# Bias rows stored from ScalarE's queue, with new priorities of a planned order, in a transformer block on one core

## The chip, the cores and the metric

The kernel runs on one core of a Trainium2 chip. The metric is the device time of one execution in microseconds. A core has TensorE (PE, matmuls and transposes), VectorE (DVE), ScalarE (ACT), GpSimd (POOL) and SyncE (SP); SP does nothing here but issue DMA transfers. ACT and POOL can issue transfers too.

## The reference

One layer on a sequence of 512 tokens with 1024 features, in float32. A first product with `w_in` gives the inputs of two attentions: MLA with low-rank latents, and NSA with compressed, selected and sliding branches. Then follow the output product, a gated FFN and a last norm.

```python
u = rmsnorm(h, norm_mix_g[l]) @ w_in[l]
c_q, c_kv, k_rope, q_nsa, kv_cmp, kv_slc, kv_win, gate_logits = jnp.split(u, cuts, axis=-1)
o_mla = mla_mixer(c_q, c_kv, k_rope, ...)
o_nsa = nsa_mixer(q_nsa, kv_cmp, kv_slc, kv_win, gate_logits, ..., t5_table)
mixed = jnp.concatenate([rmsnorm(o_mla, ...), rmsnorm(o_nsa, ...)], axis=-1)
h = h + mixed @ w_out[l]
f = rmsnorm(h, norm_ffn_g[l])
h = h + (jax.nn.silu(f @ w_gate[l]) * (f @ w_up[l])) @ w_down[l]
```

In NSA each head adds a bias to its scores that depends on the distance of query and key alone; it is looked up in `t5_table`, 32 buckets by 8 heads. The bias rows of this document are that lookup. The compressed branch makes 31 keys and values per group by a small network, `gelu(blk @ w1) @ w2`, over windows of 32 tokens.

## The kernel before, in words

**Arithmetic.** Each float32 operand is split into a high and a low part (`split`, `split_pieces`), and a product is three matmuls (`mm3`, L167 to L170): high by high, low by high, high by low. A weight tile is therefore loaded (`w_raw`), cast to its high part (`w_hi`, L391) and subtracted to its low part (`w_lo`, L393 on DVE or L394 on POOL) before PE can use it. `weight` (L396) does this: there are two buffers for `w_raw` and three for the parts, so a load waits until the tile two before it is split.

**Stages.** x and the weights of the latents come first; x is normed and transposed in four blocks of 128 tokens (`xTh`, `xTl`), and each block gives its latents (`latent`, L461), the matmuls of 440 columns. Then come the projections from x with 512 columns: keys (two, k0 and k1), queries (four, q0 to q3), the raw inputs of the compressed keys and values, and the values. For the compressed keys and values, pieces of the projection go to `rr`, the hidden layer is a product with two tiles of `w1` (L715, L717), its sum passes through `hs` and `z` (L728 to L748) to `hth` and `htl` (L391, L393), and these meet `w2h`. The softmax of the heads follows, then MLA, the output product and the FFN.

**The bias rows.** `bias_rows` (L529) multiplies `choice`, a one-hot table of buckets, with the split `t5_table` (`tx`, split into `txp`), negates the result into `brow` (L539) and stores it in DRAM. Two stores of 8 x 32 x 320 values, the row of each head written 32 times, make `ldr` (L543, 320 KB each); two small ones make `gdr` (L545). From there the rows are loaded again, skewed: `bn` for each pair of heads in four loads (L595), and `ga` for the compressed branch in eight (L603). All these go through SP's queue.

**The order.** Nothing is left to a scheduler at run time: `Plan` (L74) is given jobs with an engine, an estimated time, the jobs that they follow, a priority, and the buffers that they take and free. `run` places each job on its engine in its own model of time, the lower priority number first among those that could start at once, and emits the instructions in that order. The numbers in `PRI` (L123) shift the priorities of whole groups. So a small change of a number moves instructions on several engines. `sum_weights` (L1344) adds tiles of `w_down` for the FFN beside all this: ACT issues a copy into T (L1356), POOL an accumulating transfer onto it (L1357).

The queries' results (`qs`) leave their PSUM bank by ACT (high part) and DVE (low part, L370); there are two such banks, named mm.

Of the kernel before, what the change touches and what calls it, by code (L numbers as in the profile page):

```python
# [13 lines left out]
OP = mybir.AluOpType  # L14
# [9 lines left out]
H = 8  # L24
# [30 lines left out]
class Plan:  # L55
# [11 lines left out]
    def add(self, ways, fn=None, after=(), pri=0.0, takes=(), frees=(), lag=None):  # L67

        if fn is not None:
            ways = [(ways[0], ways[1], fn)]  # L70
        j = Job(ways, [a for a in after if a is not None], pri, takes, frees, lag)
        self.jobs.append(j)
        return j
# [13 lines left out]
    def run(self):  # L87
        busy = {}
        clock, ready, waiting = {"dma": 3500.0, "dma2": 3000.0}, [], list(self.jobs)
        while waiting or ready:  # L90
# [29 lines left out]

PRI = dict(k0=-28.1, q0=-12.1, v=-4.9, ck=-13.0, k1=8.9, cv=-9.5, q1=-9.4, q2=57.6, q3=12.2, mla=56.1, out=231.6, slack=0, pdve=18.6, ppool=86.3,  # L123
           pact=287.7, wload=-5.7, wsplit=39.6, mkeys=-41.5, lat=-40.5, cmp=-18.2, cuse=34.2, use=6.8, sout=44.8, seven=181.5, xoff=-24.0,
           xstep=-81.5, loff=-30.6, woff=-18.0, wstep=8.6)


@with_exitstack
def block_kernel(ctx: ExitStack, tc: tile.TileContext, I, out):
    nc = tc.nc  # L130
    ve, se, pe, gp, sy = nc.vector, nc.scalar, nc.tensor, nc.gpsimd, nc.sync
# [103 lines left out]
    ldr = dram.tile([H, 32, 640], F32, name="ldr")  # L235
    gdr = dram.tile([H, 1008], F32, name="gdr")
# [21 lines left out]
    tx = p0.tile([33, H], F32, name="tx")  # L258
    choice = kqv.tile([33, 1648], F32R, name="choice", tag="kl")
    txp = p0.tile([33, 2, H], F32R, name="txp")  # L260
# [2 lines left out]
        q.dma_start(xt[0][:, 512 * e:512 * e + 512], xv[:, 0, 512 * e:512 * e + 512])  # L263
    se.dma_start(grow, I["norm_mix_g"].unsqueeze(0))
    ve.memset(tx, -BIG)


    order = tc.manual_schedule(engines={e.engine for e in (ve, se, pe, gp)})
# [2 lines left out]
    add = plan.add  # L271
# [117 lines left out]
    def split_pieces(h, l, raw, n, after, pri, takes=(), frees=()):  # L389

        j = add([("act", t_act(n, True), lambda: se.copy(h(), raw())), ("dve", t_copy(n), lambda: ve.tensor_copy(h(), raw()))],  # L391
                None, after, pri, takes=takes)
        return add([("dve", t_dve(n), lambda: ve.tensor_tensor(l(), raw(), f(h()), op=OP.subtract)),  # L393
                    ("pool", t_pool(n), lambda: gp.tensor_tensor(l(), raw(), f(h()), op=OP.subtract))], None, [j], pri, frees=frees)  # L394
# [32 lines left out]
    g_row = add(("dma2", 20), lambda: None, pri=-99, lag=600)  # L427
# [6 lines left out]
    wl_ready = []  # L434
    for u in range(4):
        j = add(("dma", 1300), lambda u=u: load_wl(u), pri=-97 + (u if u < 3 else 4), lag=950)
# [6 lines left out]
    def load_small():  # L443
        sy.dma_start(rc, I["rope_c"].rearrange("(t p) d -> p t d", p=P))
        sy.dma_start(rs, I["rope_s"].rearrange("(t p) d -> p t d", p=P))
        sy.dma_start(rowv, I["row_valid"])
        sy.dma_start(tx[0:32, :], I["t5_table"])
        sy.dma_start(og[:, 0:4], I["out_norm_mla_g"].rearrange("(k p) -> p k", p=P))
        sy.dma_start(og[:, 4:8], I["out_norm_nsa_g"].rearrange("(k p) -> p k", p=P))

    small = add(("dma", 2100), load_small, pri=-89.5, lag=950)
    choice_in = add(("pool", 1010), lambda: gp.dma_start(choice, I["bias_choice"]), pri=-89.5, lag=3400)
# [76 lines left out]
    def bias_rows(c0, c1):  # L529
        d = {}  # L530

        def product():
            d["o"] = bank("tp")
            for e in range(2):
                pe.matmul(d["o"][0:H, 0:c1 - c0], txp[:, e], choice[:, c0:c1], start=e == 0, stop=e == 1)

        def negated():
            d["row"] = pa.tile([H, S], F32, name="brow", tag="s", bufs=4)[:, 0:c1 - c0]
            se.mul(d["row"], d["o"][0:H, 0:c1 - c0], -1.0)  # L539

        def out():
            if c1 <= 640:
                sy.dma_start(ldr[:, :, c0:c1], d["row"].unsqueeze(1).to_broadcast([H, 32, 320]))  # L543
            else:
                sy.dma_start(gdr[:, c0 - 640:c1 - 640], d["row"])  # L545

        j = add(("pe", (c1 - c0) * 0.834), product, [table, choice_in], -60, takes=["tp"])
        choice_used.append(j)
        j = add(("act", t_act(c1 - c0)), negated, [j], -60, takes=["s"], frees=["tp"])
        return add(("dma", 950 if c1 <= 640 else 100), out, [j], -60, frees=["s"], lag=4300)  # L550

    table = split_pieces(lambda: txp[:, 0], lambda: txp[:, 1], lambda: tx, H, [small], -60)
    choice_used = []
    bias0 = [bias_rows(0, 320), bias_rows(320, 640)]
    bias1 = [bias_rows(640, 1144), bias_rows(1144, 1648)]
# [526 lines left out]
    for t in range(NT):  # L1082
        d = {}
# [6 lines left out]
        j = add(("pe", 640), go, uv_ready + lat_done, mpri + t, takes=["mm"])  # L1090
        vm_ready += split_values(lambda t=t: late["vm"][:, t], lambda d=d: d["o"].rearrange("p (h d) -> p h d", h=H), S, [j], mpri + t)
    for q in range(2):
        qc = slice(384 * q, 384 * q + 384)
        for t in range(NT):
            pri = mpri + 4 + 4 * q + t
            d = {}
# [15 lines left out]
            j = add(("pe", 480), lambda go=go: go(0), [uq_ready[q][0]] + lat_done, pri, takes=["mm"])  # L1112
            j = add(("pe", 480), lambda go=go: go(1), [j, uq_ready[q][1]], pri)
            j = add(("act", t_act(256)), lambda qd=qd, ov=ov: se.copy(qd()[:, :, 0:64], ov()[:, :, 0:64]), [j], pri)
            j = add(("dve", 480), rope, [j], pri, frees=["mm"])
# [192 lines left out]
    for nh in range(2):  # L1308
        for t in range(NT):
            d = {}  # L1310
# [14 lines left out]
    for nh in range(2):  # L1325
        for t in range(NT):
            d = {}
# [6 lines left out]
            j = None  # L1334
            for k in range(4):
                j = add(("pe", 640), lambda k=k, go=go: go(k), [j, wo[4 + 2 * nh + k // 2][1][k % 2]] + latent_jobs, 300 + 4 * nh + t,
                        takes=["mm"] if k == 0 else (), frees=["part2"] if t == NT - 1 and k % 2 else ())
# [6 lines left out]
    def sum_weights():  # L1344
        wd = I["w_down"].rearrange("(q j p) (n c) -> p q j n c", j=2, p=P, n=2)
        last = [ga_loaded]
        for u in range(6):
            qs = slice(2 * u, min(2 * u + 2, 11))
            n = qs.stop - qs.start
            for name in ("T1", "T3", "T2", "T4"):  # L1350
                wsum[name, u] = dram.tile([P * n, 512], F32, name=f"{name}_{u}")
            b = lambda jj, nn, qs=qs: wd[:, qs, jj, nn, :]
            o = lambda name, u=u: wsum[name, u].rearrange("(q p) c -> p q c", p=P)
            for name, first, second in (("T1", lambda b=b: b(0, 0), lambda b=b: b(0, 1)), ("T3", lambda b=b: b(1, 1), lambda b=b: b(0, 1)),
                                        ("T2", lambda b=b: b(0, 0), lambda o=o: o("T3")), ("T4", lambda b=b: b(1, 0), lambda o=o: o("T2"))):
                j = add(("act", 80), lambda o=o, name=name, first=first: se.dma_start(o(name), first()), last, 900, lag=8000)  # L1356
                j = wsum_done[name, u] = add(("pool", 1000), lambda o=o, name=name, second=second: gp.dma_start(o(name), second(), accum_op=OP.add, max_dma_last_dim=2048), [j], 900, lag=8500)  # L1357
                last = [j]

    sum_weights()  # L1360
# [580 lines left out]
```

## Time and profile before

| | before |
|---|---|
| time, median of 3 runs | 654.06 us (652.67 to 654.91) |
| the profiled execution | 651.38 us, span 649.6 us |
| mean granted TensorE clock | 0.983 of full |
| PE busy | 611.7 us, 94% of the span |
| DVE busy | 524.7 us, 81% |
| ACT busy | 370.0 us, 57% |
| POOL busy | 175.9 us, 27% |
| chain that ended last | PE 76%, DVE 14% |

The span runs from the first to the last instruction; the execution is some 1.8 us longer. Busy time is time in instructions of the engine itself; issues of transfers are rows of the engine's queue (SPq, ACTq). Overlapping matmuls are drawn with their modelled ends, so a row's length is more than the distance to the next one. In a timeline, the bracket at the end of a row gives the idle time ahead of it and what ended it.

### The profile page before, as it was taken

What the parts mean: (1) busy time and instruction counts of PE and PEld (TensorE: products, weight loads), DVE (VectorE), ACT (ScalarE), POOL (GpSimd) and SP (SyncE); (2) the same over time, 40 slices, a digit from 0 to 9 for tenths busy, and PEclk for the clock granted to TensorE, in tenths of its full rate; (3) what the DMA queues carried; (4) which work ended last, traced back from release to release, by engine and by line L of the source; (5) the groups of instructions that cost most, each with busy time, mean ns of one, the idle gap of its engine ahead of it and who ended that gap; (6) DMA issues with size and microseconds to landing.
All of it is one profiled execution on the core that took longest, in us unless ns stands there. A gap on an engine that the chain in (4) does not pass through costs nothing.

```text
span 649.6 us, 11224 instructions
## 1 busy us (share of the span) xinstructions
PE 611.7 (94%) x3973; PEld 543.9 (84%) x3973; DVE 524.7 (81%) x1078; ACT 370.0 (57%) x766; POOL 175.9 (27%) x253
## 2 busy tenths in 40 slices
PE   5998599998998999999999999999999999999994
PEld 3877488887897777787999999999999998888883
DVE  5947377799999888858987778977778899978846
ACT  4532134798898877526644554455455576558434
POOL 5622236356975475434100000000000000000003
PEclk9999789999999989999999999999999999999998
DMA  8526564327323555456775775557553466455503
GB/s 277 133 52 136 144 153 93 63 68 179 65 35 70 185 173 123 101 154 197 170 201 160 195 190 135 138 156 195 163 149 108 112 212 199 146 174 191 186 1 130
DMA packets 76297, 92.75 MB, mean 143 GB/s; under 512 B 10240, under 2 KB 49584, under 8 KB 76242
## 3 DMA queue, kind: packets, MB, share of 16 engines
q1 hardware_dynamic: 63856, 68.22, 34.7%
q0 software_dynamic: 6080, 11.75, 11.6%
q10 hardware_dynamic: 6306, 12.06, 5.8%
q8 instruction: 31, 0.51, 0.3%
q14 instruction: 24, 0.20, 0.1%
HBM read 89.24 MB, written 25.85 MB: 177 GB/s over the span
## 4 chain that ended last, share of the span: by engine, by line
PE 76%; DVE 14%; issue 3%; ACT 3%; DMA 1%; POOL 1%; SPq 1%; POOLq 0%; ACTq 0%; DVEq 0%
PE mm L168 10%; PE mm L169 10%; PE mm L170 10%; PE sc L170 7%; PE sc L169 7%; PE sc L168 7%; PE pv L879 3%; PE pv L170 3%; PE pv L169 3%; PE pv L168 3%; PE tp L845 3%; PE sc L1185 2%; PE tp L169 2%; PE tp L170 2%; PE tp L168 2%
## 5 line engine op out<-in xcount | busy, mean ns | idle before, releaser
L170 PE MATMUL sc<-fh,w_unit 128*128 128x256 f32 x352 | 98.5, 280 | 0.0
L168 PE MATMUL sc<-fh,w_unit 128*128 128x256 f32 x352 | 98.5, 280 | 0.0
L169 PE MATMUL sc<-fl,w_unit 128*128 128x256 f32 x352 | 98.2, 279 | 0.0
L1396 DVE TENSOR_TENSOR w_unit<-b_raw,w_unit 128x1024 fp32r<-128x1024 f32 (+1 forms) x54 | 63.8, 1182 | 25.5 <-ACT w_unit L1580 15.2
L169 PEld LDWEIGHTS sc<-fl,w_unit 128*128 128x128 f32 x352 | 66.2, 188 | 0.0
L170 PEld LDWEIGHTS sc<-fh,w_unit 128*128 128x128 f32 x352 | 66.1, 188 | 0.0
L168 PEld LDWEIGHTS sc<-fh,w_unit 128*128 128x128 f32 x352 | 65.8, 187 | 0.0
L834 ACT ACTIVATE s<-s,m 128x128 f32<-128x128 f32 (+3 forms) x96 | 53.5, 558 | 11.3 <-DVE m L829 10.5
L1396 DVE TENSOR_TENSOR w_unit<-b_first,w_unit 128x1024 fp32r<-128x1024 f32 (+1 forms) x34 | 40.0, 1176 | 24.6 <-ACT w_unit L1580 18.2
L840 POOL TENSOR_SCALAR s<-s,l,gates 128x128 f32<-128x128 f32 (+3 forms) x64 | 41.4, 658 | 32.2 <-DVE l L837 24.8
L170 PE MATMUL mm<-fh,w_unit 128*128 128x256 f32 x176 | 49.3, 280 | 0.0
L168 PE MATMUL mm<-fh,w_unit 128*128 128x256 f32 x176 | 49.1, 279 | 0.0
L169 PE MATMUL mm<-fl,w_unit 128*128 128x256 f32 x176 | 49.1, 279 | 0.0
L853 DVE TENSOR_TENSOR ptl<-tp,pth 128x128 fp32r<-128x128 f32 (+3 forms) x96 | 45.2, 484 | 3.9 <-ACT pth L850 3.2
L394 POOL TENSOR_TENSOR w_lo<-w_raw,w_hi 128x512 fp32r<-128x512 f32 x25 | 35.0, 1413 | 39.7 <-DVE w_hi L391 29.9
L850 ACT ACTIVATE pth<-tp 128x128 fp32r<-128x128 f32 (+3 forms) x96 | 40.4, 432 | 7.1 <-PE tp L845 6.0
L845 PE MATMUL tp<-ident,s 128*128 128x128 f32 x240 | 41.9, 280 | 2.3 <-DVE ptl L853 1.1
L1580 ACT CAST w_unit<-b_raw 128x1024 fp32r<-128x1024 f32 x32 | 33.6, 1051 | 11.8 <-issue 4.8
L1357 POOL DMA_DIRECT2D T<-T x12 | 13.2, 1100 | 100.0 <-DMA T<-in_w_down_dram 99.7
L1357 POOL DMA_DIRECT2D T<-in_w_down_dram x12 | 13.5, 1121 | 93.9 <-DMA T<-in_w_down_dram 93.9
L845 PEld LDWEIGHTS tp<-ident,s 128*128 128x128 f32 x240 | 29.0, 142 | 9.9 <-POOL s L840 4.2
L1856 POOL TENSOR_SCALAR ss<-ss 128x1 f32<-128x1 f32 x9 | 3.4, 376 | 123.3 <-ACT xo L1853 123.0
(365 smaller groups left out, 1986.1 us busy)
## 6 DMA issues: line engine op xcount, KB each, us to landing
T<-in_w_down_dram ACTq DMA_DIRECT2D x20, 512.0 KB, 5.1
b_first<-in_w_gate_dram SPq DMA_DIRECT2D x12, 512.0 KB, 4.7
b_raw<-in_w_up_dram SPq DMA_DIRECT2D x12, 512.0 KB, 6.6
T<-in_w_down_dram POOLq DMA_DIRECT2D x10, 512.0 KB, 6.4
T<-T POOLq DMA_DIRECT2D x10, 512.0 KB, 5.9
b_raw<-in_w_gate_dram SPq DMA_DIRECT2D x10, 512.0 KB, 3.9
b_late<-in_w_up_dram SPq DMA_DIRECT2D x10, 512.0 KB, 5.2
b_raw<-in_w_down_dram SPq DMA_DIRECT2D x10, 512.0 KB, 3.9
```

The lines of the kernel that those rows point to most:

```text
L168: pe.matmul(o, lh, rh, start=start, stop=False, **kw)
L169: pe.matmul(o, lh, rl, start=False, stop=False, **kw)
L170: pe.matmul(o, ll, rh, start=False, stop=stop, **kw)
L394: ("pool", t_pool(n), lambda: gp.tensor_tensor(l(), raw(), f(h()), op=OP.subtract))], None, [j], pri, frees=frees)
L834: se.activation(c["s"][:, 0:n], c["s"][:, 0:n], AF.Exp, bias=c["m"], scale=-1.0, accum_out=c["l"])
L840: eng.tensor_scalar(c["s"][:, 0:n], c["s"][:, 0:n], c["l"], gate(), op0=OP.mult, op1=OP.mult)
L845: pe.transpose(c["tp"][:, j * P:(j + 1) * P], c["s"][:, j * P:(j + 1) * P], ident)
L850: se.activation(c["dh"], c["src"], AF.Copy)
L853: ve.tensor_tensor(c["dl"], c["src"], f(c["dh"]), op=OP.subtract)
L1357: j = wsum_done[name, u] = add(("pool", 1000), lambda o=o, name=name, second=second: gp.dma_start(o(name), second(), accum_op=OP.add, max_ ...
L1396: return add(("dve", t_dve(n)), lambda: ve.tensor_tensor(dst(), a(), b(), op=op), after, pri, **kw)
L1580: j = add(("act", t_act(n, True)), lambda: se.copy(w["p"][0], b()), [rw] + need, pri + 5)
```

## The change

- `t5_table` is loaded by ACT at the start instead of by SP among the small loads, and its split no longer waits for those loads.
- The four stores of bias rows are issued by ACT (`se`) instead of SP (`sy`). In the plan each is a job of ACT, which also follows the split of the latents' weights.
- The priorities in `PRI` are replaced; those of the bias rows and of `sum_weights` become entries of it.
- The plan reckons PE's jobs below 1374 ns as 7% longer.

```diff
@@ -67,7 +67,7 @@ def add(self, ways, fn=None, after=(), pri=0.0, takes=(), frees=(), lag=None):
-            ways = [(ways[0], ways[1], fn)]
+            ways = [(ways[0], ways[1] * (1.07 if ways[0] == "pe" and ways[1] < 1374 else 1.0), fn)]
@@ -120,9 +120,9 @@
-PRI = dict(k0=-28.1, q0=-12.1, v=-4.9, ck=-13.0, k1=8.9, cv=-9.5, q1=-9.4, q2=57.6, q3=12.2, mla=56.1, out=231.6, slack=0, pdve=18.6, ppool=86.3,
...
+PRI = dict(k0=-5.4, q0=-12.1, v=51.3, ck=-13.0, k1=8.0, cv=-9.5, q1=-9.4, q2=-38.5, q3=12.6, mla=38.1, out=180.9, slack=0, pdve=20.1,
...
+           xoff=-26.6, xstep=-35.5, bias=-61.8, sums=912.1, bout=-82.5, loff=-25.8, woff=-217.5, wstep=301.5)
@@ -263,6 +263,7 @@
     ve.memset(tx, -BIG)
+    se.dma_start(tx[0:32, :], I["t5_table"])
@@ -444,7 +445,6 @@
-        sy.dma_start(tx[0:32, :], I["t5_table"])
@@ -540,16 +540,16 @@
         def out():
             if c1 <= 640:
-                sy.dma_start(ldr[:, :, c0:c1], d["row"].unsqueeze(1).to_broadcast([H, 32, 320]))
+                se.dma_start(ldr[:, :, c0:c1], d["row"].unsqueeze(1).to_broadcast([H, 32, 320]))
             else:
-                sy.dma_start(gdr[:, c0 - 640:c1 - 640], d["row"])
+                se.dma_start(gdr[:, c0 - 640:c1 - 640], d["row"])
 
-        j = add(("pe", (c1 - c0) * 0.834), product, [table, choice_in], -60, takes=["tp"])
+        j = add(("pe", (c1 - c0) * 0.834), product, [table, choice_in], PRI["bias"], takes=["tp"])
         choice_used.append(j)
         j = add(("act", t_act(c1 - c0)), negated, [j], -60, takes=["s"], frees=["tp"])
-        return add(("dma", 950 if c1 <= 640 else 100), out, [j], -60, frees=["s"], lag=4300)
+        return add(("act", 80), out, [j] + wl_ready, PRI["bout"], frees=["s"], lag=6000)
 
-    table = split_pieces(lambda: txp[:, 0], lambda: txp[:, 1], lambda: tx, H, [small], -60)
+    table = split_pieces(lambda: txp[:, 0], lambda: txp[:, 1], lambda: tx, H, [g_row], PRI["bias"])
@@ -1353,8 +1353,8 @@
-                j = add(("act", 80), lambda o=o, name=name, first=first: se.dma_start(o(name), first()), last, 900, lag=8000)
...
+                j = add(("act", 80), lambda o=o, name=name, first=first: se.dma_start(o(name), first()), last, PRI["sums"], lag=8000)
...
```

Lines 266 to 447 of the file before are one higher after the change; the rest keeps its number. No matmul is added or left out. From the mask and `w_out` on SP's order is that of before, and from the FFN's first transposes on PE's is.

On SP, between the hidden weights of the compressed keys and those of the values. Before (`w_raw<-in_w_in` is a tile of the projections):

```order
L404 DMA w_raw<-in_nsa_cmp_w_k_dram 128x8x128 x2
L543 DMA ldr<-brow 256x1x320 x2
L545 DMA gdr<-brow 8x504 x2
L404 DMA w_raw<-in_w_in_dram 128x8x128
L595 DMA bn<-ldr 32x2x512 x8
L603 DMA ga<-gdr 16x8x56 x8
L404 DMA w_raw<-in_w_in_dram 128x8x128
L404 DMA w_raw<-in_nsa_cmp_w_v_dram 128x8x128 x2
```

After the change:

```order
L405 DMA w_raw<-in_nsa_cmp_w_k_dram 128x8x128 x2
L595 DMA bn<-ldr 32x2x512 x8
L405 DMA w_raw<-in_w_in_dram 128x8x128
L603 DMA ga<-gdr 16x8x56 x8
L405 DMA w_raw<-in_w_in_dram 128x8x128
L405 DMA w_raw<-in_nsa_cmp_w_v_dram 128x8x128 x2
```

The four stores are gone from here, and the `bn` loads stand ahead of the tile of the compressed values. The tile behind the `ga` loads is that of q1 in both.

On ACT, among the norms of x (`x_109`) and the first latents. Before:

```order
L321 ACTIVATE xTh,ss<-x_109 128x4x128 x2
L362 ACTIVATE xTh<-tp 128x4x128
L321 ACTIVATE xTh,ss<-x_109 128x4x128
L362 ACTIVATE xTh<-tp 128x4x128 x2
L475 ACTIVATE cn,css<-mm 128x256
L476 ACTIVATE cn,css<-mm 128x128
L478 ACTIVATE ge<-mm 128x24
```

After the change:

```order
L322 ACTIVATE xTh,ss<-x_109 128x4x128
L543 DMA ldr<-brow 256x1x320
L322 ACTIVATE xTh,ss<-x_109 128x4x128
L363 ACTIVATE xTh<-tp 128x4x128 x2
L475 ACTIVATE cn,css<-mm 128x256
L476 ACTIVATE cn,css<-mm 128x128
L478 ACTIVATE ge<-mm 128x24
L539 ACTIVATE brow<-tp 8x320
L543 DMA ldr<-brow 256x1x320
L363 ACTIVATE xTh<-tp 128x4x128
L392 CAST w_hi<-w_raw 128x512 x2
```

Both `ldr` stores now lie here, the second ahead of a piece of x and of the first casts of projection tiles; the two `gdr` stores follow behind the last latents.

On DVE, around the hidden layer of the compressed keys. Before:

```order
L393 TENSOR_TENSOR w_lo<-w_raw,w_hi 128x512
L370 SCALAR_TENSOR_TENSOR qs<-mm,qs 64x512 x2
L689 TENSOR_SCALAR rr<-ident 128x8x2x4 x2
L391 CAST w_hi<-w_raw 128x512
L732 TENSOR_TENSOR hs<-mm,hs 128x68
L734 TENSOR_SCALAR z<-hs 128x64
L737 TENSOR_TENSOR hs<-z 128x2x32
```

After the change:

```order
L394 TENSOR_TENSOR w_lo<-w_raw,w_hi 128x512
L371 SCALAR_TENSOR_TENSOR qs<-mm,qs 64x512
L392 CAST w_hi<-w_raw 128x512
L371 SCALAR_TENSOR_TENSOR qs<-mm,qs 64x512
L394 TENSOR_TENSOR w_lo<-w_raw,w_hi 128x512
L689 TENSOR_SCALAR rr<-ident 128x8x2x4 x2
L732 TENSOR_TENSOR hs<-mm,hs 128x68
L734 TENSOR_SCALAR z<-hs 128x64
```

Of the low part's two halves of q0 (`qs`), the second now stands behind the cast of a tile, q1's. On PE the projections come in the order q2, compressed keys, q0, compressed values, q1, k0, k1, q3, values; before it was k0, compressed keys, q0, compressed values, q1, values, k1, q2, q3, with the softmax mixed in from the values on. The two small bias products stand before the transposes of x and in the first latents, where they stood behind the last latents.

## Rows read from the trace of the kernel before

**Rows 1.** The page, part 1: busy us, share of the span, instructions.

```profile
PE 611.7 (94%) x3973; PEld 543.9 (84%) x3973; DVE 524.7 (81%) x1078; ACT 370.0 (57%) x766; POOL 175.9 (27%) x253
```

**Rows 2.** Windows by stage: length; busy PE, PEld, DVE, ACT, POOL; PEclk; DMA share, GB/s.

```profile
16.00:39.00 23.00, 21.41 (x122) 19.27 (x122) 19.74 (x52) 11.08 (x35) 11.28 (x15) 1.00 0.46 117
...
62.00:92.00 30.00, 20.93 (x94) 17.11 (x94) 15.80 (x37) 5.92 (x17) 9.05 (x8) 0.77 0.56 137
92.00:312.00 220.00, 209.60 (x1297) 178.16 (x1297) 189.40 (x590) 154.26 (x427) 123.02 (x185) 0.99 0.47 121
312.00:630.00 318.00, 317.25 (x2286) 298.10 (x2285) 263.27 (x321) 173.21 (x225) 12.45 (x12) 1.00 0.56 159
```

**Rows 3.** Timeline of PE: start, length, line, operation, [idle before <- releaser].

```profile
64.22 0.76 PE L168 MATMUL mm<-xTh,w_hi 128*128 128x512 f32 x1 [1.86 <-DVE qs L370]
...
67.34 0.44 PE L169 MATMUL mm<-xTl,w_hi 128*128 128x512 f32 x1
...
78.01 0.39 PE L168 MATMUL mm<-hth,w2h 128*128 128x64 f32 x1 [6.88 <-DVE hth L391]
...
79.19 0.77 PE L168 MATMUL mm<-xTh,w_hi 128*128 128x512 f32 x1
...
84.45 0.42 PE L170 MATMUL mm<-xTh,w_lo 128*128 128x512 f32 x1
```

**Rows 4.** Timeline of SP: start and total time of the DMA issues.

```profile
40.85 1.62 SPq L543 DMA_DIRECT2D ldr<-brow  x2
43.39 8.07 SPq L545 DMA_DIRECT2D gdr<-brow  x2
51.57 3.70 SPq L404 DMA_DIRECT2D w_raw<-in_w_in_dram  x1
56.67 8.09 SPq L595 DMA_DIRECT2D bn<-ldr  x8
64.80 3.74 SPq L603 DMA_DIRECT2D ga<-gdr  x8
68.66 0.39 SPq L404 DMA_DIRECT2D w_raw<-in_w_in_dram  x1
```

**Rows 5.** Waits of SP's queue, 14 to 80 us: total, times, longest.

```profile
SPq L595 <- DMA T<-in_w_down_dram: 4.6, 1, 4.6
```

**Rows 6.** DMA from 38 to 60 us: rate in 0.55 us slices; issues, KB each, landing.

```profile
GB/s 0 0 0 0 0 0 0 14 54 44 49 54 42 54 42 51 47 49 51 42 54 44 49 47 49 51 72 54 44 49 49 47 62 145 323 342 356 177 209 216
...
w_raw<-in_w_in_dram SPq DMA_DIRECT2D x1, 512.0 KB, 8.5
...
T<-in_w_down_dram ACTq DMA_DIRECT2D x1, 512.0 KB, 4.0
```

**Rows 7.** Timeline of ACT: two stretches of it.

```profile
24.11 0.61 ACT L391 CAST w_hi<-w_raw 128x512 fp32r<-128x512 f32 x1
...
53.46 1.55 ACT L362 ACTIVATE rr<-mm 64x256 fp32r<-64x256 f32 x4 [1.23 <-PE mm L170]
...
59.01 0.69 ACTq L1356 DMA_DIRECT2D T<-in_w_down_dram  x1
```

**Rows 8.** The chain that ended last, pieces in order of time: start, length, what.

```profile
44.10 0.33 PE tp L504 x3
...
46.39 0.23 PE mm L170
...
68.66 4.02 DMA w_raw<-in_w_in_dram
...
83.37 0.43 PE mm L170
```

**Rows 9.** DMA from 14 to 36 us: rate in forty slices of 0.55 us.

```profile
GB/s 308 177 28 1 16 75 275 343 338 304 290 279 63 0 0 0 0 0 0 0 0 0 30 0 0 106 243 344 325 246 287 266 77 23 19 0 2 141 209 340
```

**Rows 10.** DMA from 60 to 82 us: issues, KB each, median landing.

```profile
T<-in_w_down_dram POOLq DMA_DIRECT2D x1, 512.0 KB, 7.0
w_raw<-in_w_in_dram SPq DMA_DIRECT2D x2, 256.0 KB, 6.5
```

More of the change, by code (lines that the diff above doesn't have):

```diff
@@ L119, in run @@
         self.jobs = []
-PRI = dict(k0=-28.1, q0=-12.1, v=-4.9, ck=-13.0, k1=8.9, cv=-9.5, q1=-9.4, q2=57.6, q3=12.2, mla=56.1, out=231.6, slack=0, pdve=18.6, ppool=86.3,
-           pact=287.7, wload=-5.7, wsplit=39.6, mkeys=-41.5, lat=-40.5, cmp=-18.2, cuse=34.2, use=6.8, sout=44.8, seven=181.5, xoff=-24.0,
-           xstep=-81.5, loff=-30.6, woff=-18.0, wstep=8.6)
+PRI = dict(k0=-5.4, q0=-12.1, v=51.3, ck=-13.0, k1=8.0, cv=-9.5, q1=-9.4, q2=-38.5, q3=12.6, mla=38.1, out=180.9, slack=0, pdve=20.1,
+           ppool=72.3, pact=310.9, wload=-10.3, wsplit=-28.4, mkeys=-2.4, lat=-20.5, cmp=-18.4, cuse=94.3, use=17.0, sout=77.2, seven=183.9,
+           xoff=-26.6, xstep=-35.5, bias=-61.8, sums=912.1, bout=-82.5, loff=-25.8, woff=-217.5, wstep=301.5)
 @with_exitstack
@@ L1355, in sum_weights @@
                                         ("T2", lambda b=b: b(0, 0), lambda o=o: o("T3")), ("T4", lambda b=b: b(1, 0), lambda o=o: o("T2"))):
-                j = add(("act", 80), lambda o=o, name=name, first=first: se.dma_start(o(name), first()), last, 900, lag=8000)
-                j = wsum_done[name, u] = add(("pool", 1000), lambda o=o, name=name, second=second: gp.dma_start(o(name), second(), accum_op=OP.add, max_dma_last_dim=2048), [j], 900, lag=8500)
+                j = add(("act", 80), lambda o=o, name=name, first=first: se.dma_start(o(name), first()), last, PRI["sums"], lag=8000)
+                j = wsum_done[name, u] = add(("pool", 1000), lambda o=o, name=name, second=second: gp.dma_start(o(name), second(), accum_op=OP.add, max_dma_last_dim=2048), [j], PRI["sums"], lag=8500)
                 last = [j]
```

## The prediction

> **What bounds the kernel now.** I read the page's engine totals first. PE is busy 611.7 us of a span of 649.6 [rows 1], so the question is where the other 38 us lie and which of them this change can reach. The windows by stage answer it [rows 2]. From 312 to 630 us PE works 317.25 of 318 us at the full clock; nothing can be won there unless matmuls go away, and none does. From 92 to 312 us, where the softmax stands, PE idles 220 - 209.60 = 10.4 us while DVE is busy 189.40. The stretch from 62 to 92 us is the bad one: PE works 20.93 of 30 us, and at a mean granted clock of 0.77.
>
> PE's timeline says what happens in that stretch [rows 3]. PE waits 1.86 us for a bank that DVE has to empty (`qs`), and after the projection of the compressed values it waits 6.88 us for `hth`, the hidden layer of the compressed keys. With a short third wait of 0.33 us these are the stretch's 30 - 20.93 = 9.07 us. After either wait the matmuls run at the lower level of the clock, 1.2 GHz. The chain shows 0.43 us for a matmul of 512 columns there and 0.23 us at 2.4 GHz [rows 8]. The first slow spell lasts from 64.22 to 67.34 us, 3.12 / 0.43 = 7 matmuls, which lose 0.20 us each: 1.45 us. The second, from 79.19 to 84.45 us, loses 5.26 / 0.43 x 0.20 = 2.45 us. **The stretch loses 9.07 + 1.45 + 2.45 = 13.0 us.**
>
> Why is `hth` late? Not for its own work. On DVE the cast of the next weight tile, that of q1, stands ahead of the steps that make `hth`, and the tile came late. The chain runs through its transfer: issued at 68.66 us, 4.02 us long [rows 8], landed at 72.7 us, and `hth` reaches PE at 78.01 us [rows 3], 5.3 us behind it. SP's timeline tells why it was issued so late [rows 4]. Two `ldr` stores go out at 40.85 us; the two `gdr` stores behind them hold SP for 8.07 us although they are small; the tile after them holds it 3.70 us, where a free issue takes 0.39 us. Then eight `bn` loads hold it 8.09 us, in which the fifth waits 4.6 us for a transfer T that it does not read [rows 5]: transfers share a set of completion counters in turn, and the issue waits until the counter's last user has landed. Eight `ga` loads take 3.74 us, 0.47 us each. While the stores drain, from 42 to 55 us, the DMA engines move some 42 to 54 GB/s, and the tile issued at 51.57 us lands only after 8.5 us [rows 6].
>
> **The change, part by part.**
>
> *Stores off SP's queue.* SP loses four issues, and with them the holds behind them. In the new order the `bn` loads follow the two halves of the compressed keys' hidden weights. They can go once the last latent block is through, at 44.10 + 0.33 = 44.4 us [rows 8]. An issue takes (8.09 - 4.6) / 8 = 0.44 us [rows 4, 5], so all eight are out by 47.9 us if the stores have landed by then. The next tile, the compressed values', goes between 47.9 and 51.6 us, since its buffer comes free as before. Four `ga` loads follow. The fifth `ga` load now waits for the first T, which is the wait to watch. T stands on ACT behind the four `rr` pieces, which end at 53.46 + 1.55 = 55.0 us, and lands 4.0 us later [rows 6, 7]: 59.0 us. Four more issues of 0.47 us give 60.9 us for the tile of q1, against 68.66 us. With the same 4.02 us it lands at 64.9 us, **7.8 us earlier**.
>
> *What is late next.* DVE's new order puts the second low half of `qs` behind the cast of that tile; before, it stood ahead of it. This half empties the bank that the compressed values' projection takes. So this wait grows: tile 64.9 us, plus about 0.43 us for the cast and 0.6 us for `qs` (an estimate from ACT's 0.61 us for a piece of that size [rows 7]), gives 66.0 us, and PE has been out of work since 64.22 - 1.86 = 62.4 us. It idles 3.6 us and then loses 1.45 us to the clock, as now. The projection's 24 matmuls at 0.23 us end at 66.0 + 5.5 + 1.45 = 73.0 us. The chain to `hth` is through at 64.9 + 5.3 + 0.6 = 70.8 us, 2.2 us before PE asks, so the wait of 6.88 us and the second cold spell go. What stays is 3.6 + 1.45 = 5.1 us. **Gain: 13.0 - 5.1 = 7.9 us.** Its ends are 0 (the tile as late as now) and 13.0 us (no wait left).
>
> *Stores on ACT's queue.* ACT gains five issues, the table among them. Its nearest issue takes 0.69 us [rows 7], so 3.5 us in all; ACT is busy only 11.08 of 23 us from 16 to 39 us [rows 2], and I cost them at nothing. Without this cover they would cost 3.5 us. What speaks against it is that a store may hold the issuing engine as `gdr` held SP, about 4 us each [rows 4]. That happened behind `ldr` stores still draining. By my walk the first `ldr` store now goes at about 16.5 us and the second at 22.5 us, each with half of the 14 us that both take at the rate of [rows 6], and the `gdr` stores go at 41 to 43 us into an idle queue. I take no hold; one hold would cost ACT 4 us.
>
> *The table earlier, four bias products earlier.* The products are the same. The first pair now stands before PE's first transposes of x. I take 0, within 1 us either way.
>
> *The order of projections.* q2 comes first, then keys and q3 before the softmax, with the values' products spread into it. Counts are the same. Against the 10.4 us that PE idles there [rows 2] I take 0, and 4 us either way, which is 4/10 of that row. From the FFN's first transposes on, PE's order is the same: 0. The factor 1.07 on PE's costs and the priority of the sums act only through the order.
>
> The profiled execution took 651.38 us, 2.7 us less than the median of 654.06. The sum made on it is 651.38 - 7.9 = 643.5 us; on the scale of the median **654.06 - 7.9 = 646.2 us**. A difference of 0.3% is 2 us here, about what a measurement can tell from no change.
>
> **The queue against the bytes.** The tile of 51.57 us moved hardly anything until the stores ahead of it in the same queue had drained: the rate stays near 50 GB/s to 55 us and jumps past 320 GB/s after 56 us [rows 6]. So the queue cost the time, and another queue should save it. The Trainium skill speaks against this kind of change: its page "DMA: Bandwidth & Descriptors", section "Issuing engines are not separate DMA queues", says that transfers from whichever engine run on the same 16 DMA engines and interleave, and that issuing from several saves only the sequencers' issue time. The trace before cannot decide it, since it has no large store on one queue beside a tile on the other. By that rule the sum is the third rival's.
>
> **Rivals.** *T takes the stores' place (same).* T may be slower: another one took 7.0 us beside tiles that took 6.5 us [rows 10]. Then the tile lands 3.0 + 2.5 = 5.5 us later, at 70.4 us; PE idles from 62.4 to 71.5 us, 9.1 us, and loses 2.45 us to the clock. Gain 13.0 - 11.6 = 1.4 us: 652.6 us. For it: T stands right in front of the fifth `ga` load. Against it: on ACT, in this very place, T took 4.0 us.
>
> *Stores hold back the first tiles (slower).* On ACT the casts of the second projection tile stand, in order, ahead of the pieces of x that PE needs next; the last casts before them run now at 24.11 us [rows 7]. The tiles land now by 21 us at 300 GB/s [rows 9], and the stores now come into this stretch. If the second tile lands at 32 us instead, ACT stands 32 - 24.1 = 7.9 us, PE with it, and the clock costs 2.45 us on top: 10.4 - 7.9 = 2.5 us slower, 656.6 us. It decides from a landing of about 31.5 us on. For it: a tile took 8.5 us next to the stores [rows 6]. Against it: that was in the same queue; half of these bytes have moved before the store starts; 8.5 us would still land at 25 us, and the DMA engines idle from 21 to 26 us [rows 9].
>
> *Only the issue time is saved (same).* If the stores still drain when the `bn` loads want their data, SP waits as now and saves four issues of 0.44 us: 1.8 us, 652.3 us. Against it: 14 us of drain from 16.5 or 22.5 us end well before 44.4 us.
>
> *The middle stage moves.* The values' products inside the softmax could fill PE's idle time there, or DVE, busy 189.40 of 220 us [rows 2], could fall behind. Half of 10.4 us either way: 641 or 651.4 us; a loss of over 10 us there would make the whole slower.
>
> **How the numbers follow.** The forecast with its own spread (641 to 650 us) has 0.52, the middle stage's better half, down to 638 us, 0.12; T in the stores' place 0.11; the issue time alone 0.06; the stores holding back tiles 0.09; the middle stage losing more than the gain 0.06; smaller losses that leave 650 to 652 us 0.04. Faster takes the forecast, the better middle and the last: 0.68. Same takes T and the issue time: 0.17. Slower takes the remaining two: 0.15. The range of 638 to 655 us leaves out about 0.05 below and 0.13 above.
>
> **What would show it.** Right: SP issues the tile of q1 near 61 us; PE waits some 3.6 us for `qs` near 62 us, and no 6.88 us for `hth`; the hidden layer of the values is done 8 us earlier; the stores run between 17 and 31 us while SP's tiles there land as now. Wrong: PE idle between 24 and 32 us behind ACT's casts; the fifth `ga` load waiting on T past 60 us; idle of PE above 14 us after 92 us; or issues on ACT of 3 us and more.

## The result, and the profile after

The changed kernel takes 642.88 us, the median of 4 runs (642.63 to 645.58), against 654.33 us before (652.67 to 654.91, also 4 runs): the ratio is 0.9838, with a 95% interval of 0.9807 to 0.9870. So it is faster by 11.4 us, or 1.6%, and the interval leaves out 1. The forecast was 646.2 us, a gain of 7.9 us, within a range of 638 to 655 us. The profiled execution took 642.98 us, span 641.1 us; against the one of before, 651.38 us, that is 8.4 us less. The difference between 8.4 and 11.4 us is taken up below, with the start.

The page's busy times of the changed kernel, to set beside [rows 1]:

```profile
PE 609.1 (95%) x3973; PEld 540.8 (84%) x3973; DVE 520.9 (81%) x1078; ACT 369.6 (58%) x767; POOL 177.0 (28%) x252
```

PE's busy time falls by only 2.6 us; the other 5.9 us by which the span is shorter are idle time of PE. In windows cut by stage, the busy time falls by 3.4 us from the end of the compressed keys' hidden layer to the end of the values' (20.33 to 16.89 us, with the granted clock up from 0.77 to 0.91) and grows by 2.1 us in the start, up to the last latents (36.14 to 38.23 us).

The windows by stage, the columns as in [rows 2]:

```profile
16.00:39.00 23.00, 22.09 (x115) 19.07 (x114) 18.65 (x50) 11.43 (x37) 12.18 (x16) 1.00 0.63 123
62.00:92.00 30.00, 26.36 (x147) 22.52 (x145) 24.26 (x53) 9.19 (x23) 11.04 (x10) 0.94 0.63 161
92.00:312.00 220.00, 211.38 (x1341) 180.10 (x1342) 186.95 (x582) 160.56 (x437) 125.14 (x184) 1.00 0.48 122
312.00:630.00 318.00, 317.26 (x2250) 296.51 (x2249) 262.99 (x323) 171.67 (x228) 13.82 (x17) 1.00 0.54 154
```

The stage from 62 to 92 us works 26.36 of 30 us at a granted clock of 0.94, where it was 20.93 us at 0.77. In the other three windows PE's busy time moves by less than 2 us.

PE's timeline there, beside [rows 3]:

```profile
67.86 0.77 PE L168 MATMUL mm<-xTh,w_hi 128*128 128x512 f32 x1 [2.42 <-DVE qs L371]
...
70.98 0.41 PE L169 MATMUL mm<-xTl,w_hi 128*128 128x512 f32 x1
...
73.91 0.19 PE L168 MATMUL mm<-hth,w2h 128*128 128x64 f32 x1
...
86.06 0.72 PE L925 MATMUL sc<-kc,qs 128*128 128x64 f32 x5 [1.01 <-DVE qs L371]
```

One wait for `qs` is left, 2.42 us; the slow spell behind it lasts from 67.86 to 70.98 us; the product with `hth` at 73.91 us carries no bracket, so PE did not wait for it. The scores at 86.06 us wait 1.01 us for another half of `qs`.

SP's timeline, beside [rows 4], and its wait for T, beside [rows 5]:

```profile
28.96 0.37 SPq L405 DMA_DIRECT2D w_raw<-in_w_in_dram  x1
...
48.42 3.65 SPq L595 DMA_DIRECT2D bn<-ldr  x8
53.41 0.39 SPq L405 DMA_DIRECT2D w_raw<-in_w_in_dram  x1
53.90 8.66 SPq L603 DMA_DIRECT2D ga<-gdr  x8
62.67 0.39 SPq L405 DMA_DIRECT2D w_raw<-in_w_in_dram  x1
```

```profile
SPq L603 <- DMA T<-in_w_down_dram: 5.0, 1, 5.0
```

The tile of q1 goes out at 62.67 us instead of 68.66, although the latents before it were through 3.8 us later than before. The eight `ga` loads take 8.66 us, of which 5.0 us are the fifth one's wait for T. The issue at 28.96 us takes 0.37 us, although the second `ldr` store is still draining, now in ACT's queue.

ACT's timeline, with the issues that it now makes, beside [rows 7]:

```profile
17.39 0.85 ACTq L543 DMA_DIRECT2D ldr<-brow  x1
...
24.09 0.71 ACTq L543 DMA_DIRECT2D ldr<-brow  x1
...
36.43 0.62 ACT L392 CAST w_hi<-w_raw 128x512 fp32r<-128x512 f32 x1 [3.53 <-DMA w_raw<-in_w_in_dram]
...
44.98 0.30 ACTq L545 DMA_DIRECT2D gdr<-brow  x1
...
46.24 0.27 ACTq L545 DMA_DIRECT2D gdr<-brow  x1
...
56.54 0.38 ACT L363 ACTIVATE rr<-mm 64x256 fp32r<-64x256 f32 x1 [4.18 <-PE mm L170]
56.55 0.69 ACTq L1356 DMA_DIRECT2D T<-in_w_down_dram  x1
56.93 1.16 ACT L363 ACTIVATE rr<-mm 64x256 fp32r<-64x256 f32 x3
```

No store holds ACT: the issues take 0.85, 0.71, 0.30 and 0.27 us. T is issued at 56.55 us, 0.01 us behind the start of the first of four `rr` pieces.

The rate of transfers from 14 to 36 us in slices of 0.55 us, beside [rows 9]:

```profile
GB/s 374 325 205 61 22 140 294 313 337 322 290 287 161 49 54 44 51 42 51 47 47 54 44 51 42 51 47 49 54 78 149 210 236 83 127 168 278 328 269 156
```

The stores drain from 21 to 31 us, for the most part at 42 to 54 GB/s; of this stretch 21 to 26 us were idle before.

To compare kernels, I cut each profile at four points on PE: A ends where the last transposes of a latent block start (L505), B with the last product of the compressed keys' hidden layer, C with the last one of the compressed values' (L717), D where the FFN's first transposes start, and E with the span. The numbers are differences of these start times, in us.

| kernel | A | B | C | D | E | profiled run | median |
|---|---|---|---|---|---|---|---|
| before | 44.26 | 17.85 | 29.41 | 210.5 | 347.6 | 651.38 | 653.3 to 654.3 |
| changed | 48.02 | 17.18 | 19.28 | 210.1 | 346.6 | 642.98 | 642.88 |
| e1, stores on ACT only | 46.77 | 23.09 | 23.94 | 215.7 | 347.8 | 659.19 | 658.97 |
| e2, old priorities | 44.91 | 17.85 | 22.52 | 211.8 | 347.6 | 646.47 | 645.43 |
| e3, stores on SP | 52.65 | 17.16 | 19.28 | 211.5 | 346.4 | 648.85 | 649.44 |
| e4, changed, T by POOL | 47.76 | 17.17 | 18.77 | 210.6 | 346.6 | 642.67 | 643.26 |
| e6, e4 and qs first | 48.14 | 17.17 | 17.39 | 210.9 | 346.6 | 642.00 | 641.45 |
| e10, e6 and spread rows | 48.91 | 17.16 | 17.37 | 210.2 | 346.4 | 641.82 | 642.10 |
| e9, before, spread rows | 47.67 | 17.85 | 24.90 | 212.5 | 347.6 | 652.28 | 648.96 |
| e11, before, T by POOL | 45.30 | 17.86 | 26.32 | 211.3 | 348.0 | 650.57 | 650.38 |
| e12, before, both | 45.27 | 17.85 | 17.33 | 212.8 | 347.6 | 642.57 | 642.57 |
| e13, e1 and spread rows | 48.16 | 17.85 | 25.49 | 217.1 | 347.6 | 658.11 | 654.28 |

C is the stage of the forecast. It shrinks by 10.1 us from before to after; A grows by 3.8 us, of which 0.69 us are three matmuls of a projection that the new order has there and not in B. Ratios below are to runs of before taken beside each kernel. One run of e10 was slow, 854.79 us at a granted clock of 0.656, and its median is that of the other four.

### The profile page after: what moved, and what is told of

It is laid out like the page before. It is cut to its first block, busy times and chain, and to the rows that moved or that the text cites. A ratio compares the mean times of both kernels' runs of the same rounds, so it can differ in the third digit from the quotient of the medians.

```text
span 641.1 us, 11228 instructions
## 1 busy us (share of the span) xinstructions
PE 609.1 (95%) x3973; PEld 540.8 (84%) x3973; DVE 520.9 (81%) x1078; ACT 369.6 (58%) x767; POOL 177.0 (28%) x252
## 3 DMA queue, kind: packets, MB, share of 16 engines
q1 hardware_dynamic: 63248, 67.53, 34.2%
## 4 chain that ended last, share of the span: by engine, by line
PE 71%; DVE 13%; issue 5%; ACT 4%; DMA 3%; POOL 2%; SPq 0%; POOLq 0%; ACTq 0%; DVEq 0%
PE mm L168 9%; PE mm L170 9%; PE mm L169 9%; PE sc L170 7%; PE sc L169 7%; PE sc L168 7%; PE pv L169 3%; PE pv L170 3%; PE pv L168 3%; PE tp L845 3%; DMA w_raw<-in_w_in_dram 2%; PE pv L879 2%; DVE s L829 2%; DVE ptl L853 2%; PE tp L168 1%
## 5 line engine op out<-in xcount | busy, mean ns | idle before, releaser
L834 ACT ACTIVATE s<-s,m 128x128 f32<-128x128 f32 (+3 forms) x96 | 53.6, 559 | 11.7 <-DVE m L829 11.2
L1396 DVE TENSOR_TENSOR w_unit<-b_first,w_unit 128x1024 fp32r<-128x1024 f32 (+1 forms) x34 | 40.0, 1175 | 24.4 <-ACT w_unit L1580 18.1
L850 ACT ACTIVATE pth<-tp 128x128 fp32r<-128x128 f32 (+3 forms) x96 | 39.0, 431 | 7.9 <-PE tp L845 4.7
L845 PE MATMUL tp<-ident,s 128*128 128x128 f32 x240 | 40.5, 277 | 2.2 <-DVE ptl L853 1.6
L1580 ACT CAST w_unit<-b_raw 128x1024 fp32r<-128x1024 f32 x32 | 33.6, 1051 | 11.4 <-PE pv L169 5.9
L845 PEld LDWEIGHTS tp<-ident,s 128*128 128x128 f32 x240 | 27.4, 140 | 9.7 <-POOL s L840 3.5
```

What stands on the lines that cost most here:

```text
L834: se.activation(c["s"][:, 0:n], c["s"][:, 0:n], AF.Exp, bias=c["m"], scale=-1.0, accum_out=c["l"])
L845: pe.transpose(c["tp"][:, j * P:(j + 1) * P], c["s"][:, j * P:(j + 1) * P], ident)
L850: se.activation(c["dh"], c["src"], AF.Copy)
L1396: return add(("dve", t_dve(n)), lambda: ve.tensor_tensor(dst(), a(), b(), op=op), after, pri, **kw)
L1580: j = add(("act", t_act(n, True)), lambda: se.copy(w["p"][0], b()), [rw] + need, pri + 5)
```

## The experiments

**First four: which part carries the gain?** e1 makes one part of the change alone:

```diff
-sy.dma_start(ldr...); sy.dma_start(gdr...)
+se.dma_start(ldr...); se.dma_start(gdr...)
-return add(("dma", 950 if c1 <= 640 else 100), out, [j], -60, frees=["s"], lag=4300)
+return add(("act", 80), out, [j] + wl_ready, -60, frees=["s"], lag=6000)
```

> The kernel before with one part of the change: the four stores go to ACT's queue, as jobs of ACT; table, priorities and costs as before, so the stores stay at 40 to 45 us. Theory 'early stores': the ldr rows still land near 55 us, and now four bn loads stand ahead of the tile of the compressed values, so that tile goes out near 58 us instead of 51.6 and the tile of q1 near 66 us or later; no gain, 653 to 659 us. Rival 'the queue alone': SP's holds of 8.07 and 3.3 us are all that matters, the tile of q1 goes out near 58 us and the time falls to 645 to 649 us. In both, the gdr issues take 0.3 to 4 us each on ACT; 4 us would show that a store holds whichever engine issues behind ldr.

Measured: 658.97 us, ratio 1.0081 (1.0059 to 1.0102), slower, at the upper end of the first theory's range. SP's waits and one row of ACT's issues:

```profile
SPq L595 <- DMA ldr<-brow: 23.1, 1, 23.1
```

```profile
46.05 8.28 ACTq L545 DMA_DIRECT2D gdr<-brow  x2
```

The `bn` loads, four of them now ahead of a tile, wait 23.1 us for the `ldr` rows, and PE with them: B is 5.2 us longer. C is 5.5 us shorter, so up to its end nothing is won. That e1 is slower, and not merely no faster, goes with D, 5.2 us longer in another order of products (see e13), and not with the drain; A's 2.5 us lie within what the start varies by. The two small `gdr` issues hold ACT for 8.28 us, just as they held SP for 8.07 us [rows 4]: in both kernels the engine that issues behind undrained `ldr` stores in the same queue is held. So another queue alone, with the stores as late as before, gives nothing.

e2 takes the changed kernel back to the old `PRI` table and drops the 7%:

```diff
-PRI = dict(k0=-5.4, ..., bias=-61.8, sums=912.1, bout=-82.5, ...)
+PRI = dict(k0=-28.1, ..., bias=-60, sums=900, bout=-60, ...)
-ways[1] * (1.07 if ...
+ways[1] * (1.0 if ...
```

> The changed kernel with the old priorities and without the 7%: stores on ACT, table early. The first ldr store goes near 16 us, the second near 41 us, so the bn loads start near 49 us. T does not stand ahead of the ga loads in the rotation here. Theory: the gain hangs on SP being free of the stores and on the tile of q1, which goes out near 58 us; PE's wait of 6.9 us for hth goes, 644 to 648 us. Rival 'the new priorities carry the gain': the time stays at 651 us or more. The start should lose less than the 3 us that the changed kernel lost if the new order of the splits is to blame, and as much if the early table is.

Measured: 645.43 us, ratio 0.9879 (0.9855 to 0.9903). The early table and the stores on ACT bring most of the gain without the new priorities. The tile of q1 goes out at 62.10 us and not at 58, and PE still waits 2.6 us for `hth`: C is 3.2 us longer than in the changed kernel, D 1.7, E 1.0 and B 0.7, and A is 3.1 us shorter. A, 44.91 us, lies within what the order of before shows (44.26 to 48.16 us) and below the 47.76 us and more of the new order, which speaks for the new order and against the early table as what the start costs; but it is one profile, and the start varies, as said below.

e3 is the changed kernel with `sy` in the place of `se` in both stores, everything else and the place of the stores kept.

> The changed kernel with the four stores on SP's queue again, at the early place that the plan gives them. Theory 'the queue counts': the tiles behind each ldr store wait in SP's queue until it has drained (7 us each), issues behind them take about 4 us as gdr's did, and ACT's casts and PE wait in the first 45 us; 646 to 651 us. Rival 'only the early place counts': 642 to 645 us, like the changed kernel. The Trainium skill's rule on issuing engines would give the rival's time, less the issue time of four stores.

Measured: 649.44 us, ratio 0.9943 (0.9923 to 0.9964): 6.6 us above the changed kernel, within the first theory's range. SP's timeline around the two `ldr` stores, one of its waits, the landing of the tiles from 23 to 34 us, and PE's wait:

```profile
12.06 0.86 SPq L543 DMA_DIRECT2D ldr<-brow  x1
...
13.52 4.07 SPq L447 DMA_DIRECT2D rowv<-in_row_valid_dram  x1
...
23.42 0.73 SPq L543 DMA_DIRECT2D ldr<-brow  x1
24.20 4.49 SPq L405 DMA_DIRECT2D w_raw<-in_w_in_dram  x2
28.79 3.24 SPq L691 DMA_DIRECT2D posr<-in_nsa_cmp_pos_v_dram  x1
```

```profile
SPq L405 <- POOL w_lo L395: 3.6, 1, 3.6
```

```profile
w_raw<-in_w_in_dram SPq DMA_DIRECT2D x2, 512.0 KB, 9.6
```

```profile
35.71 0.90 PE L504 MATMUL tp<-ident,cn 128*128 128x128 f32 x3 [4.87 <-DVE xTl L369]
```

Behind the first `ldr` store one issue takes 4.07 us, behind the second one 3.24 us. The row of 4.49 us is no such issue: it holds two, of 0.47 and 0.37 us, and a wait of 3.6 us for a buffer between them; but a tile issued there lands only after 9.6 us. PE waits 4.87 us in the transposes of the latents, and A is 4.6 us longer. C is 19.28 us, that of the changed kernel: so C's gain comes with the early place of the stores and the new order, and does not need the other queue. What the other queue gives, as long as the rows drain slowly, stands in the start. The Trainium skill, in "DMA: Bandwidth & Descriptors", section "Issuing engines are not separate DMA queues", says that several issuing engines only save the time to issue, and calls this time usually small. Here single issues take 3.24 and 4.07 us; how much of the 6.6 us is issue time and how much the late landing behind the store, the run does not separate.

**e4: the wait that took the place.** The changed kernel with the first copy into T on POOL:

```diff
-lambda o=o, name=name, first=first: se.dma_start(o(name), first())
+lambda ..., q=gp if (name, u) == ("T1", 0) else se: q.dma_start(o(name), first())
```

> The changed kernel with the first copy into T issued by POOL instead of ACT; nothing else moves on PE, DVE and SP, but the fifth ga load no longer waits for T. Theory: the tile of q1 goes out near 58.5 us instead of 62.67, the second low half of qs is ready before PE asks, the wait of 2.42 us and the slow clock behind it (1.45 us) go; 638.5 to 641 us. Rival 'another wait takes T's place' (the buffer of the tile, a ga load): the tile goes out after 61 us, 642 to 644 us.

Measured: 643.26 us, ratio 0.9848 (0.9824 to 0.9872), no gain over the changed kernel. The theory was right on the tile and wrong on what it is worth. Issue of the tile on SP, then PE's wait, then DVE's work ahead of it:

```profile
58.69 0.39 SPq L405 DMA_DIRECT2D w_raw<-in_w_in_dram  x1
```

```profile
66.95 0.62 PE L168 MATMUL mm<-xTh,w_hi 128*128 128x512 f32 x1 [1.78 <-DVE qs L371]
```

```profile
64.02 0.68 DVE L371 SCALAR_TENSOR_TENSOR qs<-mm,qs 64x512 fp32r<-64x512 f32 x1
64.73 1.35 DVE L392 CAST w_hi<-w_raw 128x512 fp32r<-128x512 f32 x1
66.11 0.69 DVE L371 SCALAR_TENSOR_TENSOR qs<-mm,qs 64x512 fp32r<-64x512 f32 x1
```

The tile leaves 4.0 us earlier, and PE still waits 1.78 us: on DVE the first half of `qs` starts only at 64.02 us, then comes the cast, which takes 1.35 us here, and then the half that PE needs. DVE's own order had become the limit. e6 adds that the cast of q1's tile follows the `qs` of q0 (`[j] + list(need)` with `need=q_ready[0]` in `weight`):

> As e4_first_sum_on_POOL, and on DVE both low halves of q0 (qs) stand ahead of the cast of q1's tile again, as before the change. In e4 the tile went out at 58.69 us as forecast, and yet PE waited 1.78 us for qs: DVE's own row of work, the cast with its 1.35 us included, ends last there. Theory 'order on DVE': the wait falls to 0.5 us or less and most of the slow clock behind it goes (1.45 us), 640 to 642 us. Rival 'DVE is simply full' (the work ahead of both halves ends at 64.0 us whatever the order): the wait shrinks and another one, for hth, takes its place, 642.5 to 644 us.

Measured: 641.45 us, ratio 0.9806 (0.9769 to 0.9844). The time is within the theory's range. The wait falls to 0.4 us, and another of 1.2 us, for `hth`, comes in its place, as the rival said; C is still 1.4 us shorter than in e4. The interval overlaps that of the changed kernel, so I do not call it faster.

**e9, e11, e12: is the new order needed at all?** e9 takes the kernel before and changes only how the `ldr` rows leave: the split table holds each head 16 times, so the product has each row on 16 partitions, 128 in all.

```diff
-txp = p0.tile([33, 2, H], F32R, name="txp")
+txp = p0.tile([33, 2, H, 16], F32R, name="txp")
-sy.dma_start(ldr[:, :, c0:c1], d["row"].unsqueeze(1).to_broadcast([H, 32, 320]))
+sy.dma_start(ldr.rearrange("h (r k) c -> (h r) k c", k=2)[:, :, c0:c1], d["row"].unsqueeze(1).to_broadcast([P, 2, 320]))
```

> The kernel before, stores still on SP at 40 us, but the two ldr products give each head's row on 16 partitions (128 instead of 8) and each store writes every row twice from there; same bytes. Theory 'the stores drain slowly because 8 partitions feed them': both are through within 2 to 3 us instead of 14, the gdr issues take 0.4 us each instead of 4, and SP is free at 45 us. The tile of q1 then waits in the rotation for T alone, which ACT issues near 59 us: it goes out near 63.1 us instead of 68.66, PE's wait for hth falls from 6.88 us to some 1.5 us, 646 to 649 us. Rival 'the rate belongs to DRAM or to these rows': unchanged, 652 to 655 us.

Measured: 648.96 us, ratio 0.9925 (0.9903 to 0.9946), at the end of the theory's range. SP's timeline, its wait, the transfers from 38 to 60 us (rate in slices of 0.55 us; KB each, median landing), and what is left of PE's wait for `hth`:

```profile
44.12 1.64 SPq L546 DMA_DIRECT2D ldr<-brow  x2
46.80 0.76 SPq L548 DMA_DIRECT2D gdr<-brow  x2
...
66.71 0.39 SPq L404 DMA_DIRECT2D w_raw<-in_w_in_dram  x1
```

```profile
SPq L404 <- DMA T<-in_w_down_dram: 4.3, 1, 4.3
```

```profile
GB/s 189 295 295 73 0 0 0 0 0 0 0 0 0 191 358 286 349 36 29 19 238 261 197 0 0 0 0 0 0 0 57 166 315 352 325 205 261 213 209 129
...
ldr<-brow SPq DMA_DIRECT2D x2, 320.0 KB, 2.6
```

```profile
76.60 0.27 PE L168 MATMUL mm<-hth,w2h 128*128 128x64 f32 x1 [3.43 <-DVE hth L391]
```

The same bytes that drained at 42 to 54 GB/s from 8 partitions [rows 6] go at 286 to 358 GB/s from 128, and the two `gdr` issues take 0.76 us together instead of 8.07. The tile then waits 4.3 us for T alone, and PE 3.43 us for `hth`, where 1.5 us were expected. The Trainium skill's page "DMA: Bandwidth & Descriptors", section "Rules for kernel authors", says that an outermost dimension below 16 confines a transfer to at most that many DMA engines. The busy share of the 16 DMA engines agrees: it is 0.40 to 0.50 from 42 to 56 us in the kernel before, where the stores have 8 partitions. The rates go further than this rule: twice the engines would double the rate, and it rose some seven times. What else holds a store from 8 partitions back, no run here separates.

e11 makes e4's edit in the kernel before:

> The kernel before with the first copy into T issued by POOL; nothing else moves. No bn load waits for T. If the stores and T share the blame for the late tile, it goes out near 64 us (bn loads from 56.7 us, 16 issues of 0.45 us behind them) instead of 68.66, and the time falls by 4 to 6 us, 647.5 to 650 us. If T alone were to blame, the tile would go out below 60 us and the time fall by 8 us or more; if the stores alone, nothing changes.

Measured: 650.38 us, ratio 0.9950 (0.9931 to 0.9969); SP's timeline:

```profile
44.43 7.98 SPq L545 DMA_DIRECT2D gdr<-brow  x2
...
57.70 3.61 SPq L595 DMA_DIRECT2D bn<-ldr  x8
...
65.29 0.39 SPq L404 DMA_DIRECT2D w_raw<-in_w_in_dram  x1
```

and PE's wait for `hth`:

```profile
75.66 0.39 PE L168 MATMUL mm<-hth,w2h 128*128 128x64 f32 x1 [5.66 <-DVE hth L391]
```

The `gdr` issues hold SP as before, the `bn` loads do not wait for T any more, and the tile leaves at 65.29 us. So the stores and T share the blame, as expected; but 2.9 us are gained, where 4 to 6 were forecast.

e12 has both edits in the kernel before:

> The kernel before with both edits, the spread ldr rows on SP's queue and the first copy into T by POOL: neither stores nor T hold SP, with the order of before on PE and DVE, the stores on SP and the table late. The tile of q1 goes out near 58 us, the wait of 6.88 us and the second slow spell (2.45 us) go: 643 to 646 us, as good as the changed kernel. Rival 'the change won through its new order': 648 us or more.

Measured: 642.57 us, ratio 0.9824 (0.9790 to 0.9859), the time of the changed kernel and a little below the forecast range. SP's timeline, and the waits that are left on PE:

```profile
44.40 0.76 SPq L548 DMA_DIRECT2D gdr<-brow  x2
...
59.81 0.39 SPq L404 DMA_DIRECT2D w_raw<-in_w_in_dram  x1
```

```profile
63.73 0.47 PE L168 MATMUL mm<-xTh,w_hi 128*128 128x512 f32 x1 [0.37 <-DVE qs L370]
...
70.34 0.30 PE L169 MATMUL mm<-htl,w2h 128*128 128x64 f32 x1 [1.13 <-DVE htl L393]
```

The tile leaves at 59.81 us. C is 17.33 us. With the stores at their old place on SP's queue, the table late and the old priorities, the gain is the whole gain. Against the 653.27 us of the runs of before beside them, taking away the stores' hold alone gives 4.3 us (e9), T's alone 2.9 us (e11), both 10.7 us. In SP's queue the two holds simply add up: counted from point A, the tile goes out after 24.4 us in the kernel before, 19.0 in e9, 20.0 in e11 and 14.5 in e12, so 5.4 and 4.4 us are saved one by one and 9.9 together. On PE they do not add up. With one hold left PE still waits 3.43 or 5.66 us for `hth`, and the mean granted clock of C is 0.79 or 0.81, hardly above the 0.77 of before; with none left the longest wait is 1.13 us and the clock is 1.00.

**e10 and e13.** e10 puts e9's rows into e6.

> The changed kernel with three edits: first copy into T by POOL, both low halves of qs ahead of the cast (e6), and the ldr rows on 128 partitions (e9). What is left for the third edit: in the changed kernel the stores drain from 21 to 31 us, and the third projection tile lands 3.5 us after ACT asks for it, behind which PE waits 0.9 us for a latent block. Theory: this wait goes, 0.5 to 1.5 us below e6, 639.5 to 641 us. Rival: the wait was hidden or the start hangs on other transfers: 641 to 642.5 us, like e6.

Measured: 642.10 us, ratio 0.9822 (0.9800 to 0.9844): the rival's time. ACT's wait of 3.53 us for a late tile, which the changed kernel shows at 36.43 us, is gone from the trace, but A is not shorter (48.91 us).

e13 puts e9's rows into e1.

> As e1_stores_only (stores of the kernel before on ACT's queue at 40 us, 659 us), with the ldr rows on 128 partitions. If e1 lost through the drain of its stores, the bn loads, which stood until 59.35 us there, go out near 47 us, the gdr issues take ACT under 1 us each instead of 4, and the time falls to that of e9 (649 us) or a little below: 646 to 650 us. Then the queue makes no difference once the rows drain fast. Rival 'the queue counts for itself': 3 us or more below e9, 643 to 646 us.

Measured: 654.28 us, ratio 1.0024 (1.0003 to 1.0045). A miss of 4 us: the drain is cured (B is 17.85 us again), 4.7 us less than e1's 658.97 us, but the tile waits for T as in e9,

```profile
SPq L404 <- DMA T<-in_w_down_dram: 4.7, 1, 4.7
```

and D is 217.1 us, as it was 215.7 us in e1, where four profiles with the order of before have 210.5 to 212.8. In both the stores are jobs of ACT, and PE's order of products in D is the same in the two and another than before. PE idles 11.7 us there in e1 and 10.9 in e13 against 9.3 before, and is busy 2.7 and 4.9 us longer, at a mean granted clock of 0.98 and 0.96 against 0.99. Which step of the new order does it stays open; and since D moved too, e13 does not settle whether the queue counts once the rows drain fast.

## Why the prediction was right

- **What bounds the kernel: right.** The stretch from 62 to 92 us was the place: C is 10.1 us shorter, D and E by 1.4 us together; only the start is longer.
- **The tile goes out earlier, and the fifth `ga` load's wait for T is what stands in front of it: right,** with 5.0 us of wait. The forecast was 60.9 us, measured 62.67, but with the latents 3.8 us later. Counted from there it came 2 us sooner than forecast. 0.7 us of it are the matmuls moved from B to A; the term that was off is T's issue, 1.5 us: I had it behind the end of the four `rr` pieces, behind which it stands in the program, but it goes out 0.01 us after the first of them has started. An issue on ACT did not wait here until the instructions ahead had finished.
- **PE's wait for `qs` grows, that for `hth` goes: right.** Forecast 3.6 us and a slow spell of 1.45 us; measured 2.42 us and (70.98 - 67.86) / 0.43 x 0.20 = 1.45 us. What the waits and the slow clock lose is 3.9 us instead of 13.0; 9.1 us gained against 7.9 forecast. One step was counted too kindly: PE comes to `hth` behind 18 of the projection's 24 matmuls, not behind all, so by the forecast's own terms the margin was 0.8 us and not 2.2. It held.
- **Stores on ACT cost nothing: right** in the changed kernel, whose issues take 0.27 to 0.85 us. In e1, with the stores in the other place, they hold ACT for 8.28 us.
- **The start, 0 within 1 us: wrong by the profile, by less in the runs.** A is 3.8 us longer, 3.1 us without the moved product. But the profiled execution of before had the shortest start of all that share its order in A (before, e12, e11, e1, e9 and e13): 44.26, 45.27, 45.30, 46.77, 47.67 and 48.16 us. Against their middle, 46.0 us, the change costs about 48.0 - 0.7 - 46.0 = 1.3 us, an estimate. The 1.8 us by which that execution lies below the middle would be the larger part of the 3.0 us between 8.4 us (profiles) and 11.4 us (medians), and of the 2.7 us by which my sum, made on it, stood below the median; with one profile of each kernel this is argued and not shown.
- **The middle stage, 0 within 4 us: right,** D is 0.4 us shorter. The FFN's stage E, forecast 0, is 1.0 us shorter.
- **The size was in part luck.** Between the profiles the gain is 8.4 us and the forecast was 7.9, but the parts are 10.1 us less in C, 0.7 in B and 1.4 in D and E, and 3.8 us more in A: what C gave beyond the forecast and what the start took nearly cancel.
- **The rivals.** T did take the stores' place, but sooner than I feared and landing after 4.3 us instead of 7.0, so that it cost little; e4 shows that behind it stands DVE's order. The stores' drain did make a tile late (3.53 us on ACT), and e10, where that wait is gone, is no faster for it. "Only the issue time is saved" falls with the changed kernel's own trace: the stores have drained by 31 us, and the `bn` loads at 48.42 us do not wait for their data.

So the gain in C does come from SP being free of slow stores earlier, as argued, although T still holds SP for 5.0 us. That a gain of this size needs another queue, new priorities or the early table does not follow, and e12 shows that it does not: there SP is free because the stores drain fast.

## What to carry to other kernels

When a store feeds from few partitions, look at the issues behind it in the same queue: their length, not the store's, shows what it costs, and spreading the source over 128 partitions may be cheaper than moving queues. Two holds in a row can add up in the queue and yet give little on PE one by one, as long as a wait and the slow clock behind it remain; so undo both before judging either. And compare profiles by stages of the same work, with more than one profile of the same code, before a few microseconds of one stage are given a cause.

## What was not expected of the hardware

PE's same sequence of products up to point A varied by 3.9 us over the six profiles. In e1 the matmuls of 440 columns still take 0.72 us at 20.02 us and 0.36 us from 22.05 us on; in the kernel before the last long one starts at 13.64 us and the short ones begin at 17.22 us. The granted clock reads 1.00 in the window from 12 to 24 us in both. PE's rows in e1:

```profile
20.02 0.72 PE L168 MATMUL mm<-pth,xTh 128*128 128x440 f32 x1
...
22.05 0.36 PE L168 MATMUL mm<-wl,xTh 128*128 128x440 f32 x1
```

The six profiles fall into two groups by this. Where the last matmul of 440 columns with over 0.6 us starts at 13.6 to 14.7 us (before, e11, e12), A ends 32.2 to 32.3 us after the first one has started; where it starts at 20.0 to 21.2 us (e1, e9, e13), 34.2 to 34.3 us. The rest of the 3.9 us is the start of the first one itself, 12.11 to 13.83 us. What makes the fast rate come sooner or later stays open.
